# Second layer of a two-layer encoder: one 48-row product for the meta tokens' values of both halves, and two steps of the second half's norm issued one step later

## The chip, the cores and the metric

The kernel runs on one core of a Trainium2 chip. The metric is the device time of one execution in microseconds (us); the median of several runs is given.

## The reference

An encoder of two layers is applied to two requests (256 and 512 tokens of width 1024), each with the same 16 meta tokens put in front. Layer 0 mixes tokens by latent attention, layer 1 by windowed attention with 16 query heads in 4 groups; each is followed by a squared-ReLU MLP. Cut to what the change touches, the mixer of layer 1:

```python
qkv = x @ w_qkv                                   # x: 16 meta tokens + S tokens, width 1024
q = partial_rope(qkv[..., :1024]); k = partial_rope(qkv[..., 1024:1280]); v = qkv[..., 1280:]
km, vm = k[:, :16], v[:, :16]                     # meta keys and values: every query sees them
for each block of 128 queries:                    # own keys: 128 before to 128 after
    s = q_b @ [km, k_b].T / 8 + mask
    p = exp(s - m) / (sum(exp(s - m)) + exp(sink - m))
    out_b = p @ [vm, v_b]
```

Ahead of it stands the layer norm that ends layer 0: `y = (h - mean) * rsqrt(mean((h - mean)**2) + eps) * g + b`.

## The kernel before

All 800 columns (tokens of both requests, and the 16 meta tokens twice) are kept transposed, features on partitions, in two halves `hf` of 400 columns. Half 0 has its meta tokens in columns 0 to 15, half 1 in columns 128 to 143. Products are made in three matmuls each (`mm3`, lines 445 to 448): an operand is split into a high and a low part, and high x high, high x low and low x high are added in PSUM. The high part is a cast on ACT (L749, weights L761), the low part a subtraction on DVE (L751, weights L763).

The function `attention1` writes down the work from the last down-projection of layer 0's MLP to the output projection of layer 1 as tasks with a rough cost each; a list scheduler (`Plan`) puts them into an order for each engine by these costs, and each engine runs its list strictly in that order. So taking out or moving one task can shift others on any engine. In order:

- `down`: the down-projection's last part; PE, then DVE adds it to `acc` (L2094), and the sum over the eight feature chunks of a half, `ssb`, is gathered on POOL (L2098, L2101) and for the last two chunks on DVE (L2101).
- `layer_norm` gives three steps for each half. The mean step takes `ssb` through a product with a constant (PE L777), subtracts it (DVE L780), squares (ACT L782) and adds the squares up (POOL and DVE L786, DVE L788). The sums step brings the sums of squares onto rows (PE L795), ACT and DVE make 1/std of them (L799, L800). The scale step spreads that (PE L805), scales (DVE L810, ACT L813) and writes the halves' input `H[hf]` (`hb`) as high (ACT L749) and low part (DVE L751).
- `rope("q", c, hf, w)` projects a chunk `c` of queries in four steps of two feature chunks and turns it (DVE L2138, L2141, POOL L2143, DVE L2146, then the split L749 and L751) into `Q` (`q`); `rope("k", ...)` likewise for keys.
- `values(hf, wv)`: values of blocks of 128 tokens ("b", into `V`) and of the 16 meta tokens ("m", into `Vm`), 24 matmuls of 256 columns each. Here the activations are the stationary operand, so a product has as many rows as tokens. `Vm` gets its rows by four small copies on ACT (L2175) for each half.
- Attention in 24 items (head chunk `cp`, block `b`): `scores` (PE L2213, DVE L2222 adds the mask and takes maxima, L2230 and L2233, ACT L2237 exponentials with sums, L2240, DVE L2241, L2242, L2254, L2266 and POOL L2264 for two of four rows of heads each), `transposes` (PE L2283, L2291, ACT L2284, L2295), `outputs` (PE L2309, L2316). Names carry the item: `sma01` are the probabilities of `cp` 0, block 1; `es01` and `rs01` its sink exponentials and sums, `pk01` its meta columns. Beside the first items run the second half's values and the query chunks that are left.

PSUM has eight banks `wb_0` to `wb_7` in this stretch, taken in turn. The planned order of the norm steps is set in the loop that calls them:

Of the kernel before, what the change touches and what calls it, by code (L numbers as in the profile page):

```python
# [19 lines left out]
P = 128  # L20
D = 1024
NT = 800
META = 16
HALF = 400
# [349 lines left out]
def tile_encoder(ctx: ExitStack, tc: tile.TileContext, ins: dict, y):  # L374
    nc = tc.nc
    V, S, G = nc.vector, nc.scalar, nc.gpsimd
# [26 lines left out]
    def ps_w(name):  # L403
        return bank("w", name)
# [40 lines left out]
    def mm3(out, lh, ll, rh, rl, start, stop, **kw):  # L445
        nc.tensor.matmul(out, lh, rh, start=start, stop=False, **kw)  # L446
        nc.tensor.matmul(out, lh, rl, start=False, stop=False, **kw)  # L447
        nc.tensor.matmul(out, ll, rh, start=False, stop=stop, **kw)  # L448
# [57 lines left out]
    with ExitStack() as st:  # L506
        xp = pool("xp", side="right", stack=st)
        x = [xp.tile([P, 8, NT], F32R, tag=f"x{i}", name=f"x{i}") for i in range(2)]
# [187 lines left out]
        for o in IN_ORDER:  # L696
# [3 lines left out]
            for h in range(2):  # L700
                ps = ps_w(f"in{o}{h}")
# [11 lines left out]
                if o in (0, 1):  # L713
                    k = 2 * o + h
# [1296 lines left out]
    H = [[xs[hf].tile([P, 8, HALF], F32R, tag=f"hb{hf}{i}", name=f"hb{hf}{i}") for i in range(2)] for hf in range(2)]  # L2011
# [6 lines left out]
    at = {}  # L2018
# [41 lines left out]
    def attention1():  # L2060
        plan = Plan(
            {"wsp": NWSP, "wraw": WRAW, "wh": 1, "w": 8, "sqb": 6, "ssb": 1, "ssc": 1, "sqc": 6, "rt": 2, "sh": 1, "sma": 4, "smb": 3, "pta": 2, "ptb": 2,
             "rm": 4, "nm": 4, "rs": 4, "es": 4, "pk": 4, "ptm": 2, "mask": 1},
            {
                "wsp": spare([x for _, x in W.ready.values()]),
                "w": lambda k: ps_w(f"wb_{k}"),
                "sqb": lambda k: lnb.tile([P, HALF], F32, tag="sqb", name=f"sqb{k}", bufs=6),
                "sqc": lambda k: at["lnc"].tile([P, HALF], F32, tag="sqc", name=f"sqc{k}", bufs=6),
            },
# [42 lines left out]
        def rope(kind, c, hf, w):  # L2112
# [36 lines left out]

            return [lambda ks=ks: step(ks) for ks in (range(k, k + 2) for k in range(0, 8, 2))]  # L2150

        def values(hf, wv):

            steps = []
            for kind, i, a in [(("m", 0, 0), ("b", 0, 16), ("b", 1, 144), ("b", 2, 272)), (("b", 3, 0), ("m", 1, 128), ("b", 4, 144), ("b", 5, 272))][hf]:
                ps = new("w")
                m = META if kind == "m" else P

                def run(ps=ps, a=a, m=m):
                    for k in range(8):  # L2160
                        r = [wv[k // 4].t[:, x, (k % 4) * 256 : (k % 4 + 1) * 256] for x in range(2)]
                        mm3(ps.t[:m, :256], H[hf][0][:, k, a : a + m], H[hf][1][:, k, a : a + m], r[0], r[1], k == 0, k == 7)

                def step(kind=kind, i=i, ps=ps, run=run):
                    reads = [*wv, *both(*wv), *both(*[("H", hf, k) for k in range(8)])]
                    plan.task("PE", 24 * MM[256], run, reads=reads, writes=[ps], new=[ps], ends=[st2, st3] if hf == 0 else [st3])
                    if kind == "b":
                        plan.task("ACT", ACT(256), lambda: S.copy(at["V"][:, i], ps.t[:, :256]), reads=[ps, st1], writes=[("v", i)])
                        return
                    for ci, gi in ((0, 0), (0, 1), (1, 0), (1, 1)):  # L2170
                        x = 2 * ci + gi
                        rows = slice(32 * x, 32 * x + META)
                        src = lambda: ps.t[:META, :256].rearrange("p (a b c) -> p a b c", a=2, b=2)
                        plan.task(
                            "ACT", 290, lambda ci=ci, gi=gi, rows=rows: S.copy(at["Vm"][rows, i, :, ci, gi], src()[:, :, gi]),  # L2175
                            reads=[ps, st1], writes=[("vm", i, x)],
                        )

                steps.append(step)
            return steps  # L2180
# [245 lines left out]
        for n in range(len(ITEMS) + behind):  # L2426
            if n < len(ITEMS):
                cp, b = ITEMS[n]
# [29 lines left out]

    psum_phase(w=8)
    attention1()  # L2460
    sub.close()
    l1.close()
# [12 lines left out]
    ends = ExitStack()  # L2475
# [125 lines left out]
```

## Time and profile before

| | |
|---|---|
| median of 3 runs | 1750.49 us (1750.35 to 1751.98) |
| profiled execution | its own time is its span, 1750.7 us |
| granted PE clock, mean | 0.999 |
| busy: PE / DVE / ACT / POOL | 99% / 83% / 59% / 18% of the span |
| chain that ended last | PE 93%, DVE 4%, ACT 2% |

Rows of the profile in order of time give the start (us from the span's start), the duration, engine, line, operation, output<-inputs, shapes and, in brackets, how long the engine was idle ahead of it and whom it waited for. A PE row writes rows x columns: `128*16 128x256` has a stationary operand of 128 by 16 and a moving one of 128 by 256. Matmuls are pipelined, so a matmul's row is longer than its distance to the next one's start.

### The profile page before, as it was taken

How to read it: one execution, taken by the hardware profiler on the slowest of the kernel's cores; microseconds unless marked ns; L12 is line 12 of the kernel's file. 1: busy time of each engine (PE TensorE's matmuls, PEld its weight loads, DVE VectorE, ACT ScalarE, POOL GpSimd, SP SyncE). 2: the span in 40 equal slices, each digit the busy share in tenths (PEclk: the TensorE clock that was granted, in tenths of full speed). 3: DMA queues.
4: the chain of work that ended last, by engine and by line, in shares of the span. 5: the costliest groups of instructions: out<-in, count | busy, mean ns of one | idle time of the engine just before them, and what ended most of it. 6: DMA issues, size and time to landing. Idle time of an engine off the chain costs nothing.

```text
span 1750.7 us, 28797 instructions
## 1 busy us (share of the span) xinstructions
PE 1732.5 (99%) x10806; PEld 1628.4 (93%) x10806; DVE 1448.0 (83%) x2937; ACT 1026.2 (59%) x2172; POOL 309.2 (18%) x290
## 2 busy tenths in 40 slices
PE   9999999999999999999999999999999999999998
PEld 9999999989999999999999998788989889988996
DVE  6998889886977898889876877876877888888877
ACT  5577777774655446545643627775665456545652
POOL 0011111112220111111103232332211111211110
PEclk9999999999999999999999999999999999999999
DMA  7211001114311221222122231021311222222222
GB/s 243 77 41 32 22 20 42 35 42 140 121 61 49 73 72 62 73 72 73 61 89 83 81 104 38 21 66 61 121 49 49 80 65 73 73 72 73 73 68 89
DMA packets 39453, 124.16 MB, mean 71 GB/s; under 512 B 4752, under 2 KB 9744, under 8 KB 39184
## 3 DMA queue, kind: packets, MB, share of 16 engines
q1 hardware_dynamic: 39312, 122.31, 21.3%
q8 instruction: 85, 1.39, 0.3%
q14 instruction: 56, 0.46, 0.1%
HBM read 119.15 MB, written 3.15 MB: 70 GB/s over the span
## 4 chain that ended last, share of the span: by engine, by line
PE 93%; DVE 4%; ACT 2%; issue 0%; DMA 0%; POOL 0%; SPq 0%; DVEq 0%; ACTq 0%
PE w L447 18%; PE w L448 18%; PE w L446 18%; PE wb L446 4%; PE wb L447 4%; PE wb L448 4%; PE wa L446 3%; PE wa L448 3%; PE wa L447 3%; PE wa L1155 2%; PE sa L446 2%; PE wa L1122 2%; PE wb L2309 2%; PE sa L448 2%; PE sa L447 2%; PE wb L2291 1%
## 5 line engine op out<-in xcount | busy, mean ns | idle before, releaser
L1734 DVE TENSOR_TENSOR acc<-acc,w 128x400 f32<-128x400 f32 (+1 forms) x306 | 184.3, 618 | 35.3 <-PE w L448 33.3
L1466 DVE TENSOR_TENSOR h<-sq,h 128x384 fp32r<-128x384 f32 (+1 forms) x164 | 94.6, 589 | 19.4 <-ACT h L1464 18.9
L446 PE MATMUL w<-h,wsp 128*128 128x400 f32 x316 | 108.9, 345 | 0.0
L447 PE MATMUL w<-h,wsp 128*128 128x400 f32 x316 | 108.9, 345 | 0.0
L447 PE MATMUL w<-h,wspi 128*128 128x400 f32 x316 | 108.9, 345 | 0.0
L446 PE MATMUL w<-h,wspi 128*128 128x400 f32 x316 | 108.7, 344 | 0.0
L448 PE MATMUL w<-h,wspi 128*128 128x400 f32 x316 | 108.7, 344 | 0.0
L448 PE MATMUL w<-h,wsp 128*128 128x400 f32 x316 | 108.6, 344 | 0.0
L1464 ACT CAST h<-sq 128x384 fp32r<-128x384 f32 (+1 forms) x164 | 82.5, 515 | 20.5 <-POOL sq L1472 19.3
L1091 POOL TENSOR_TENSOR p<-p,rs 106x512 f32<-106x512 f32 (+1 forms) x40 | 44.7, 1117 | 253.5 <-DVE pk L1082 162.2
L448 PE MATMUL w<-wspi,h 128*128 128x512 f32 (+1 forms) x182 | 71.6, 393 | 0.0
L446 PE MATMUL w<-wspi,h 128*128 128x512 f32 (+1 forms) x182 | 71.5, 393 | 0.0
L447 PE MATMUL w<-wspi,h 128*128 128x512 f32 (+1 forms) x182 | 71.5, 393 | 0.0
L1645 ACT COPY sq<-w 128x400 f32<-128x400 f32 (+1 forms) x72 | 35.0, 486 | 61.0 <-PE w L448 61.0
L1064 ACT ACTIVATE p<-sa,nm,rq 106x528 f32<-106x528 f32 (+1 forms) x80 | 63.4, 792 | 10.5 <-DVE nm L1061 4.5
L1060 DVE TENSOR_REDUCE nm<-sa 106x1 f32<-106x528 f32 (+1 forms) x80 | 56.3, 704 | 13.8 <-PE sa L448 12.4
L446 PE MATMUL w<-wsp,h 128*128 128x512 f32 (+1 forms) x170 | 67.1, 395 | 0.0
L448 PE MATMUL w<-wsp,h 128*128 128x512 f32 (+1 forms) x170 | 66.8, 393 | 0.0
L447 PE MATMUL w<-wsp,h 128*128 128x512 f32 (+1 forms) x170 | 66.7, 393 | 0.0
L446 PE MATMUL sa<-k,q 128*106 128x264 f32 (+5 forms) x208 | 63.8, 307 | 2.8 <-issue 0.9
L446 PE MATMUL w<-t,wsp 128*128 128x384 f32 (+1 forms) x176 | 60.0, 341 | 0.0
L448 PE MATMUL w<-t,wsp 128*128 128x384 f32 (+1 forms) x176 | 59.9, 341 | 0.0
(823 smaller groups left out, 6173.7 us busy)
## 6 DMA issues: line engine op xcount, KB each, us to landing
wrawo<-in_w_o_dram SPq DMA_DIRECT2D x32, 512.0 KB, 3.3
wraw0d<-in_w2b_dram SPq DMA_DIRECT2D x24, 512.0 KB, 3.3
wraw1d<-in_w2b_dram SPq DMA_DIRECT2D x18, 512.0 KB, 3.4
wrawq<-in_w_q_dram SPq DMA_DIRECT2D x8, 512.0 KB, 3.3
xr<-in_xT_dram SPq DMA_DIRECT2D x16, 200.0 KB, 3.4
wraw<-in_w_qn_dram SPq DMA_DIRECT2D x8, 384.0 KB, 3.1
wx1d<-in_w2b_dram SPq DMA_DIRECT2D x6, 512.0 KB, 3.2
out_dram<-fo SPq DMA_DIRECT2D x11, 256.0 KB, 2.0
```

The source lines that it names most:

```text
L446: nc.tensor.matmul(out, lh, rh, start=start, stop=False, **kw)
L447: nc.tensor.matmul(out, lh, rl, start=False, stop=False, **kw)
L448: nc.tensor.matmul(out, ll, rh, start=False, stop=stop, **kw)
L1060: plan.task("DVE", DVE(528), lambda: V.tensor_reduce(nm.t[:qm, 0:1], v(), axis=AX.XY, op=ALU.max, negate=True), reads=[ps], writes=[nm], n ...
L1064: lambda: S.activation(P_().rearrange("p (a b) -> p a b", b=264), v(), AF.Exp, bias=nm.t[:qm, 0:1], scale=sc, accum_out=rs.t[:qm, 0:1]),
L1091: f = lambda row=row, r=r, w=w: G.tensor_tensor(row()[:, META:T], row()[:, META:T], r().to_broadcast([qm, w]), ALU.mult)
L1122: nc.tensor.transpose(ps.t[:, k * qm : (k + 1) * qm], src[k], ident[:qm, :qm])
L1155: nc.tensor.matmul(av[64 * e : 64 * e + 64, :n], vt.t[:, k, h0 + 64 * e : h0 + 64 * e + 64], PT.t[:, e, k, :n], start=k == 0, stop=False, ...
L1464: plan.task("ACT", 530, lambda: S.copy(d.t[:, 0], c.t[:, :n]), reads=[c], writes=[(d, "hi")], new=[d])
L1466: "DVE", 570, lambda: V.tensor_tensor(d.t[:, 1], c.t[:, :n], d.t.bitcast(F32)[:, 0], ALU.subtract),
L1734: f = lambda: V.tensor_tensor(z, z, ps.t[:, : z.shape[-1]], ALU.add)
L2309: nc.tensor.matmul(av[64 * gi : 64 * gi + 64, :256], at["V"][:, kbs[k][0], gc : gc + 64], PT.t[:, a : a + 256], start=k == 0, stop=False, ...
```

## The change

Before, half 0's `values` had products for its 16 meta tokens and three blocks, and half 1's for block 3, its 16 meta tokens and two blocks. Now half 0 has only its three blocks. A new helper `meta_along` copies, on POOL, the meta columns of `H[0]` and `H[1]`, high and low part, side by side into a stretch of the query tile `Q[1]` that is not yet in use (`along`): 16 columns of half 0 and, with the 16 in between that nobody reads, 32 of half 1, 48 columns for each of eight feature chunks. One product of 48 rows makes both halves' meta values, first of half 1's list, and its eight copies on ACT fill both parts of `Vm`. The mean step of the second half's norm is issued after the first product of `values(0)` rather than the second, its sums step after the second step of query chunk 2 rather than the first, and its scale step after the fourth rather than the third; `meta_along(1)` follows it.

```diff
+        def along(x):
+            return at["Q"][1][:, x, 1, HALF : HALF + 24 * META].rearrange("p (k m) -> p k m", m=3 * META)
+
+        def meta_along(hf):
+            a, b, d = ((0, META, 0), (128 - META, 128 + META, META))[hf]
+            for x, nm in enumerate(("hi", "lo")):
+                plan.task(
+                    "POOL", POOL(8 * (b - a)), lambda x=x: G.tensor_copy(along(x)[:, :, d : d + b - a], H[hf][x][:, :, a:b]),
+                    reads=[st1, *[(("H", hf, k), nm) for k in range(8)]], writes=[("Hm", nm)], ends=[st2, st3] if hf == 0 else [st3],
+                )
...
-            for kind, i, a in [(("m", 0, 0), ("b", 0, 16), ("b", 1, 144), ("b", 2, 272)), (("b", 3, 0), ("m", 1, 128), ("b", 4, 144), ("b", 5, 272))][hf]:
+            for kind, i, a in [(("b", 0, 16), ("b", 1, 144), ("b", 2, 272)), (("m", 0, HALF), ("b", 3, 0), ("b", 4, 144), ("b", 5, 272))][hf]:
                 ps = new("w")
-                m = META if kind == "m" else P
+                m = 3 * META if kind == "m" else P
...
-                        mm3(ps.t[:m, :256], H[hf][0][:, k, a : a + m], H[hf][1][:, k, a : a + m], r[0], r[1], k == 0, k == 7)
+                        l = [along(x)[:, k] if kind == "m" else H[hf][x][:, k, a : a + m] for x in range(2)]
+                        mm3(ps.t[:m, :256], l[0], l[1], r[0], r[1], k == 0, k == 7)
...
-                    for ci, gi in ((0, 0), (0, 1), (1, 0), (1, 1)):
+                    for i, ci, gi in [(i, ci, gi) for i in range(2) for ci in range(2) for gi in range(2)]:
                         x = 2 * ci + gi
                         rows = slice(32 * x, 32 * x + META)
-                        src = lambda: ps.t[:META, :256].rearrange("p (a b c) -> p a b c", a=2, b=2)
+                        r0 = 32 * i
+                        src = lambda r0=r0: ps.t[r0 : r0 + META, :256].rearrange("p (a b c) -> p a b c", a=2, b=2)
...
         for i, f in enumerate(values(0, wv)):
             f()
-            if i == 1:
+            if i == 0:
                 mean1()
+        meta_along(0)
         for c in range(2, 8):
             w = wq(c)
             for i, f in enumerate(rope("q", c, 0, w)):
                 f()
-                if (c, i) == (2, 0):
+                if (c, i) == (2, 1):
                     sums1()
-                if (c, i) == (2, 2):
+                if (c, i) == (2, 3):
                     scale1()
+                    meta_along(1)
```

From `values` on the line numbers of the new kernel are 12 or 13 higher (L2222 becomes L2235). PE's list loses 24 matmuls. Ahead of L777 it has one product of `values(0)` instead of two; between L795 and L805 it has two steps of query chunk 2, as before, but ahead of L795 two as well instead of one. In attention the 48-row product takes the place that block 3's product had, and block 3's the place of the 16-row one; PE's list is the same from there on. The other engines' lists at the two places:

**The norm, on POOL**, around the second half's sums `ssb1`; `shq` are turned queries, `vm1` is cleared, `sqb` are squares, `q1_1` takes the meta columns. Before:

```order
L2098 TENSOR_TENSOR ssb1_9939<-acc_845 128x400
L2101 TENSOR_TENSOR ssb1_9939<-ssb1_9939,acc_845 128x400 x2
L2143 TENSOR_TENSOR shq00_9951<-shq00_9951,sin10_9551 128x384
L2101 TENSOR_TENSOR ssb1_9939<-ssb1_9939,acc_845 128x400 x2
L2029 MEMSET vm1_10023 128x1024
L786 TENSOR_TENSOR sqb4_9764<-sqb4_9764,sqb3_9761 128x400
L786 TENSOR_TENSOR sqb5_9779<-sqb5_9779,sqb1_9740 128x400
L2143 TENSOR_TENSOR shq10_10127<-shq10_10127,sin10_9551 128x384
L2143 TENSOR_TENSOR shq20_10252<-shq20_10252,sin10_9551 128x384
```

and now:

```order
L2098 TENSOR_TENSOR ssb1_9933<-acc_845 128x400
L2101 TENSOR_TENSOR ssb1_9933<-ssb1_9933,acc_845 128x400 x4
L2029 MEMSET vm1_9999 128x1024
L2143 TENSOR_TENSOR shq00_9949<-shq00_9949,sin10_9551 128x384
L2159 COPY q1_1_9993<-hb00_9545 128x8x16
L2159 COPY q1_1_9993<-hb01_9546 128x8x16
L786 TENSOR_TENSOR sqb4_9764<-sqb4_9764,sqb3_9761 128x400
L786 TENSOR_TENSOR sqb5_9779<-sqb5_9779,sqb1_9740 128x400
L2143 TENSOR_TENSOR shq10_10126<-shq10_10126,sin10_9551 128x384
L2159 COPY q1_1_9993<-hb10_9547 128x8x32
L2159 COPY q1_1_9993<-hb11_9548 128x8x32
L2143 TENSOR_TENSOR shq20_10254<-shq20_10254,sin10_9551 128x384
```

All five sums stand ahead of the first rope product now; the copies of half 0 follow it and those of half 1 stand ahead of the third.

**The norm, on DVE**, from the first rope products to the subtraction of the mean (`wsp`, `wspi` are split weights). Before:

```order
L2138 TENSOR_TENSOR rtq10_9979<-wb_6_9677,cos10_9549 128x384
L2035 TENSOR_SCALAR nsink_10028<-sink_10027 128x16
L2101 TENSOR_TENSOR ssb1_9939<-ssb1_9939,acc_845 128x400 x2
L763 TENSOR_TENSOR wsp7_792<-wrawq2_9655,wsp7_792 128x1024
L2146 TENSOR_TENSOR rtq00_9949<-rtq00_9949,shq00_9951 128x384
L763 TENSOR_TENSOR wspi41_709<-wrawq3_9823,wspi41_709 128x1024
L780 TENSOR_TENSOR acc_845<-acc_845,wb_7_9692 128x400 x6
```

and now:

```order
L2138 TENSOR_TENSOR rtq10_9979<-wb_6_9677,cos10_9549 128x384
L2101 TENSOR_TENSOR ssb1_9933<-ssb1_9933,acc_845 128x400
L2035 TENSOR_SCALAR nsink_10004<-sink_10003 128x16
L2101 TENSOR_TENSOR ssb1_9933<-ssb1_9933,acc_845 128x400
L763 TENSOR_TENSOR wsp7_792<-wrawq2_9655,wsp7_792 128x1024
L780 TENSOR_TENSOR acc_845<-acc_845,wb_5_9658 128x400 x6
```

The rope sum and the second weight split have gone behind the sums of squares (L788).

**The start of attention, on ACT**: `v1` are values, `pta` and `ptm` transposed probabilities of blocks and of meta columns. Before:

```order
L2168 COPY v1_10022<-wb_0_9568 128x256
L2237 ACT_TABLE_LOAD
L2237 ACTIVATE sma00_10695,rs00_10749<-sma00_10695,nm00_10746 128x272 x4
L2240 ACTIVATE es00_10751<-es00_10751 128x4
L2175 COPY vm1_10023<-wb_4_9641 16x2x64 x4
L2237 ACTIVATE sma01_10716,rs01_10809<-sma01_10716,nm01_10775 128x272 x4
L2168 COPY v1_10022<-wb_6_9677 128x256
L2240 ACTIVATE es01_10827<-es01_10827 128x4
L2295 COPY pta00_10837<-wb_3_9623 128x512
L2284 COPY ptm00_10848<-wb_1_9585 128x128
L2295 COPY pta00_10837<-wb_2_9603 128x512
L2237 ACTIVATE sma02_10719,rs02_10887<-sma02_10719,nm02_10829 128x272 x4
```

and now:

```order
L2188 COPY vm1_9999<-wb_7_9692 16x2x64 x8
L2250 ACT_TABLE_LOAD
L2250 ACTIVATE sma00_10668,rs00_10731<-sma00_10668,nm00_10721 128x272 x4
L2253 ACTIVATE es00_10733<-es00_10733 128x4
L2180 COPY v1_9998<-wb_3_9623 128x256
L2180 COPY v1_9998<-wb_0_9568 128x256
L2297 COPY ptm00_10798<-wb_6_9677 128x128
L2308 COPY pta00_10801<-wb_2_9603 128x512
L2308 COPY pta00_10801<-wb_3_9623 128x512
L2250 ACTIVATE sma01_10725,rs01_10830<-sma01_10725,nm01_10808 128x272 x4
L2253 ACTIVATE es01_10819<-es01_10819 128x4
L2250 ACTIVATE sma02_10723,rs02_10866<-sma02_10723,nm02_10816 128x272 x4
```

The second item's exponentials have gone behind block 4's value copy and the copies of the first item's transposes. On DVE, the first of the two scalings of the second item's rows is followed by `L2243` and `L2246` of the fourth item and by `L2254` of the third, which reads `es02`, and only then by the second scaling; before, the two scalings stood together ahead of that.

More of the change, by code (lines that the diff above doesn't have):

```diff
@@ L2150, in rope, with run @@
             return [lambda ks=ks: step(ks) for ks in (range(k, k + 2) for k in range(0, 8, 2))]
+        def along(x):
[7 more added lines that the diff above has]
+                )
         def values(hf, wv):
             steps = []
-            for kind, i, a in [(("m", 0, 0), ("b", 0, 16), ("b", 1, 144), ("b", 2, 272)), (("b", 3, 0), ("m", 1, 128), ("b", 4, 144), ("b", 5, 272))][hf]:
+            for kind, i, a in [(("b", 0, 16), ("b", 1, 144), ("b", 2, 272)), (("m", 0, HALF), ("b", 3, 0), ("b", 4, 144), ("b", 5, 272))][hf]:
                 ps = new("w")
-                m = META if kind == "m" else P
-                def run(ps=ps, a=a, m=m):
+                m = 3 * META if kind == "m" else P
+                def run(ps=ps, a=a, m=m, kind=kind):
                     for k in range(8):
                         r = [wv[k // 4].t[:, x, (k % 4) * 256 : (k % 4 + 1) * 256] for x in range(2)]
-                        mm3(ps.t[:m, :256], H[hf][0][:, k, a : a + m], H[hf][1][:, k, a : a + m], r[0], r[1], k == 0, k == 7)
+                        l = [along(x)[:, k] if kind == "m" else H[hf][x][:, k, a : a + m] for x in range(2)]
+                        mm3(ps.t[:m, :256], l[0], l[1], r[0], r[1], k == 0, k == 7)
                 def step(kind=kind, i=i, ps=ps, run=run):
-                    reads = [*wv, *both(*wv), *both(*[("H", hf, k) for k in range(8)])]
+                    reads = [*wv, *both(*wv), *both(*[("H", hf, k) for k in range(8)]), *(both("Hm", ("q", 3, 1)) if kind == "m" else [])]
                     plan.task("PE", 24 * MM[256], run, reads=reads, writes=[ps], new=[ps], ends=[st2, st3] if hf == 0 else [st3])
@@ L2169, in step @@
                         return
-                    for ci, gi in ((0, 0), (0, 1), (1, 0), (1, 1)):
+                    for i, ci, gi in [(i, ci, gi) for i in range(2) for ci in range(2) for gi in range(2)]:
                         x = 2 * ci + gi
                         rows = slice(32 * x, 32 * x + META)
-                        src = lambda: ps.t[:META, :256].rearrange("p (a b c) -> p a b c", a=2, b=2)
+                        r0 = 32 * i
+                        src = lambda r0=r0: ps.t[r0 : r0 + META, :256].rearrange("p (a b c) -> p a b c", a=2, b=2)
                         plan.task(
-                            "ACT", 290, lambda ci=ci, gi=gi, rows=rows: S.copy(at["Vm"][rows, i, :, ci, gi], src()[:, :, gi]),
+                            "ACT", 290, lambda i=i, ci=ci, gi=gi, rows=rows, src=src: S.copy(at["Vm"][rows, i, :, ci, gi], src()[:, :, gi]),
                             reads=[ps, st1], writes=[("vm", i, x)],
```

## The prediction

> **What bounds the kernel.** I read the page's first and fourth part, then PE's instructions in order of time at the two places where the change moves work, then the other engines there.
>
> The page: span, PE's row, and the shares by engine of the chain that ended last.
>
> ```profile
> span 1750.7 us, 28797 instructions
> ...
> PE 1732.5 (99%) x10806; PEld 1628.4 (93%) x10806; DVE 1448.0 (83%) x2937; ACT 1026.2 (59%) x2172; POOL 309.2 (18%) x290
> ...
> PE 93%; DVE 4%; ACT 2%; issue 0%; DMA 0%; POOL 0%; SPq 0%; DVEq 0%; ACTq 0%
> ```
>
> PE is the bound, so a product taken out is worth its spacing on PE and nothing hides it. A busy PE is modelled; the spacing of starts tells its time. What is left is small waits, and the next rows (PE in order of time, second norm of the first layer) hold one.
>
> ```profile
> 976.15 0.28 PE L446 MATMUL wb<-wspi,hb 128*16 128x256 f32 x1
> 976.27 0.28 PE L447 MATMUL wb<-wspi,hb 128*16 128x256 f32 x1
> ...
> 981.79 0.83 PE L777 MATMUL wb<-ssb,part 128*128 128x400 f32 x2
> ...
> 989.00 0.34 PE L448 MATMUL wb<-hb,wsp 128*128 128x384 f32 x1
> 990.59 0.87 PE L795 MATMUL wb<-ones,sqb 128*100 128x1 f32 x8 [1.25 <-DVE sqb L788]
> ```
>
> From 976.15 to 981.79 stand 48 matmuls, 24 with 16 rows and 24 with 128: 5.64/48 = 0.1175 us each, and 0.12 between the first two. The rows of the product do not change the spacing. L448 at 989.00 would let the next start after about 0.18; L795 (row sums of squares) starts 1.59 later, so PE waits 1.41 us for the last sum of squares (L788).
>
> **Part 1, the product that goes.** The program has 24 matmuls fewer: 24 x 0.1175 = **-2.82 us**. The 48-row product stands where a 128-row one stood; both bounds (16 and 128 rows) give 0.1175, so it costs what its neighbours do.
>
> **Part 2, the norm.** DVE and POOL in order of time, with the 16-row product still in place:
>
> ```profile
> 976.44 1.02 POOL L2143 TENSOR_TENSOR shq<-shq,sin 128x384 f32<-128x384 f32 x1 [12.77 <-DVE shq L2141]
> 977.42 2.17 POOL L2101 TENSOR_TENSOR ssb<-ssb,acc 128x400 f32<-128x400 f32 x2
> ...
> 975.29 0.56 DVE L2138 TENSOR_TENSOR rtq<-wb,cos 128x384 f32<-128x384 f32 x1 [1.59 <-PE wb L448]
> 976.82 0.67 DVE L2035 TENSOR_SCALAR nsink<-sink 128x16 f32<-128x16 f32 x1
> 979.62 1.19 DVE L2101 TENSOR_TENSOR ssb<-ssb,acc 128x400 f32<-128x400 f32 x2 [2.13 <-POOL ssb L2101]
> ...
> 982.33 1.22 DVE L763 TENSOR_TENSOR wspi<-wrawq,wspi 128x1024 fp32r<-128x1024 f32 x1
> 983.46 2.96 DVE L780 TENSOR_TENSOR acc<-acc,wb 128x400 f32<-128x400 f32 x6
> ...
> 989.96 0.57 DVE L788 TENSOR_TENSOR sqb<-sqb,sqb 128x400 f32<-128x400 f32 x1
> ```
>
> PE reaches L777 one product earlier, at 976.15 + 2.82 = 978.97. Its input was ready only at 980.8 before, because POOL's last two sums stood behind a rope product that waited 12.77 us. Now POOL makes all its sums ahead of that product, and DVE's two sums follow its rope work of 975.3 to 976.8: two of 0.6, and the small L2035 of 0.67 between, end near 978.6. So L777 does not wait, with 0.4 us to spare. DVE then has one weight split (L763, 1.22; before it stood there too, with a second one and a rope sum behind it) and starts L780 when L777 is done, near 979.9. L780's start to L788's end took 990.53 - 983.46 = 7.07, so the squares are summed at 987.0. PE has between L777 and L795 what it had, 7.39 (981.79 to 989.18), and 6 matmuls of 384 columns more, 1.05: it comes at 978.97 + 8.44 = 987.4. The wait is gone, -1.41; the margin of 0.4 is thin, and I leave 0.1 of it: **-1.3 us**. Ends: all 1.41 goes, or all of it stays.
>
> The added copies on POOL: bounds are its small MEMSET and its 384-column product of 1.02 above; I take 0.5 each, as 128 and 256 columns lie between.
>
> ```profile
> 942.32 1.05 POOL L2101 TENSOR_TENSOR ssb<-ssb,acc 128x400 f32<-128x400 f32 x1 [1.13 <-DVE acc L2094]
> 959.79 3.88 POOL L2101 TENSOR_TENSOR ssb<-ssb,acc 128x400 f32<-128x400 f32 x2 [2.16 <-DVE acc L2094]
> 1053.98 0.11 POOL L2246 MEMSET sma<- 128x16 f32 x1
> ```
>
> The same addition takes 1.05 us alone and 1.94 beside a busy DVE, so the two engines get in each other's way. The copies of the first half come just where DVE makes the last two sums; if each held DVE up by its 0.5, L777 would wait 0.6 and PE would lose that. The Trainium skill, "SBUF — State Buffer", section "Who interferes with whom", says that a VectorE instruction with two SBUF inputs and a GpSimd one that reads SBUF exclude each other for the whole instruction. By that rule, with copies as long as the 1.02 row, L777 would wait some 1.7 and the sum would lose all of the gain of this part; the trace agrees with it on POOL's side (1.94), and shows nothing of a DVE held twice in a row.
>
> The copies of the second half stand on POOL ahead of a rope product and wait for the second half's H. PE needs that half first at the 400-column matmuls, and its last pair of chunks 18 matmuls on:
>
> ```profile
> 1003.40 1.86 DVE L751 TENSOR_TENSOR hb<-acc,hb 128x400 fp32r<-128x400 f32 x2
> 1003.87 0.34 PE L446 MATMUL wb<-hb,wspi 128*128 128x400 f32 x1
> ...
> 1007.17 0.34 PE L446 MATMUL wb<-hb,wspi 128*128 128x400 f32 x1
> ```
>
> Ready at 1005.26, read at 1007.17: 1.9 to spare. PE comes 4.2 earlier. DVE comes some 2.5 to 3 earlier, since it now has three weight splits of 1.2 between L788 and the first scaling. 0.2 to 0.7 is left: 0 lost, 0.6 at worst. The rope product behind the copies is delayed by about 1 us, and the bank that it empties is wanted again eight ropes later, of some 4.2 us each: 0. On SP's queue no DMA is added; the loads of the two rope tables and some weights change places by one, and nothing in these rows waits for a landing: 0.
>
> **Part 3, the start of attention.** PE's own order there is the old one, with the 48-row product where block 3's stood and block 3's where the 16-row one stood, so its arrival times stay. ACT's and DVE's order is new. First the busy time of each engine from 1051 to 1075, then rows of ACT, DVE, POOL and PE:
>
> ```profile
> 1051.00:1075.00 24.00, 24.00 (x219) 20.77 (x219) 17.01 (x77) 18.57 (x58) 6.19 (x11) 1.00 0.07 24
> ...
> 1055.71 0.37 ACT L2168 COPY v<-wb 128x256 f32<-128x256 f32 x1 [2.65 <-PE wb L448]
> 1057.24 1.28 ACT L2237 ACT_TABLE_LOAD   x1 [1.16 <-DVE nm L2230]
> ...
> 1060.58 0.19 ACT L2240 ACTIVATE es<-es 128x4 f32<-128x4 f32 x1
> 1060.67 1.03 ACT L2175 COPY vm<-wb 16x128 f32<-16x128 f32 x4
> ...
> 1064.13 0.58 ACT L2295 COPY pta<-wb 128x512 f32<-128x512 f32 x1
> 1064.60 0.27 ACT L2284 COPY ptm<-wb 128x128 f32<-128x128 f32 x1
> 1064.76 0.61 ACT L2295 COPY pta<-wb 128x512 f32<-128x512 f32 x1
> 1065.24 0.54 ACT L2237 ACTIVATE sma<-sma,nm 128x272 f32<-128x272 f32 x1
> ...
> 1067.27 0.20 ACT L2240 ACTIVATE es<-es 128x4 f32<-128x4 f32 x1
> ```
>
> ```profile
> 1060.80 0.16 DVE L2241 TENSOR_TENSOR rs<-rs,es 128x4 f32<-128x4 f32 x1 [1.70 <-ACT es L2240]
> 1066.78 0.81 DVE L2266 TENSOR_SCALAR sma<-sma,rs 128x272 f32<-128x272 f32 x2
> 1065.93 1.24 POOL L2264 TENSOR_TENSOR sma<-sma,rs 128x272 f32<-128x272 f32 x2 [2.83 <-DVE pk L2254]
> 1063.48 1.03 PE L2291 MATMUL wb<-ident,sma 128*128 128x128 f32 x8
> 1068.46 1.04 PE L2291 MATMUL wb<-ident,sma 128*128 128x128 f32 x8
> ```
>
> PE (the first 24.00) has no gap there. *First item.* Eight copies of meta rows (8 x 0.257 = 2.06) now stand ahead of the table load, from 1055.7 to 1057.8. The load waited for DVE's maxima until 1057.2; these now come early. So the load starts at 1057.8, 0.5 later than before, and so do the exponentials and DVE's rs: 1061.3. DVE scales the rows between masks and ends near 1063.5 to 1064.0; PE's second four transposes want them at 1063.48 + 0.44 = 1063.9. I take +0.1, from 0 to 0.5.
>
> *Second item.* Its exponentials ran from 1061.7 before. Now ACT has ahead of them block 4's value copy, which waits for PE until 1063.5, and the three copies of the first item's transposes. Those take 0.47, 0.16 and 0.48 and ended at 1065.24; without the queue ahead of them at 1065.1. Four exponentials take 1067.27 - 1065.24 = 2.03, so es of item 2 is done at 1067.2 and es of item 3, straight after, at 1069.3. DVE scales one of its two rows of item 2, then has rs of item 3 in its queue, which waits for that es, and only then the other row: es to rs 0.22, scaling 0.36, near 1069.95. PE wants that row at 1068.46 + 0.44 = 1068.9. **+1.1 us** of wait where there was 0.9 to spare. Ends: 0, if PE were late anyway, and 1.7, if POOL's scaling (1.24 for two) collides too. In PE's time the third item gets the same 1.1 of respite, so I charge nothing after it; from the second item of heads on, the order is nearly as before.
>
> **The sum.** -2.82 - 1.3 + 0.1 + 1.1 = -2.9 us. The profiled span is 1750.7, so 1747.8 there; the median of the runs stands 0.2 under it (1750.49), which gives **1747.6 us**, 0.17% faster. I call 0.2% (3.5 us) what a measurement of this kernel can tell from no change.
>
> **Rivals.**
> - *Attention does not wait.* If ACT's queue is slack enough, part 3 is 0 and the time is 1750.5 - 4.1 = 1746.4. For it: PE had no gap there before, and ACT was idle for 5.4 of the 24 us. Against it: the exponentials of item 2 are bound by PE's own transposes of item 1, which no engine can hasten. 0.27.
> - *The norm's wait stays*, by copies that block DVE or a late sum: 1747.6 + 1.3 = 1748.9. The rule on the shared port gives this result. For it the margin of 0.4, against it POOL's earlier sums. 0.15.
> - *Slower.* Lateness of ACT does not heal: each item's exponentials stand behind the transposes of the one before, and each costs 1.1 again. Four items eat the 4.1 of parts 1 and 2; from the seventh on the kernel is slower by over 0.2%, and twelve give 1750.5 - 4.1 + 13.2 = 1759.6. Against it: an item is 5 us of PE and ACT's row of the span is 59%. 0.04.
>
> **How the numbers follow.** My forecast has 0.50, with 1747.0 to 1748.5 for its own range; 0.04 is for what I do not see. Low end: no wait in attention and all of 1.41, less a little, 1746.0. High end: the norm's wait stays and attention takes its upper price, 1747.6 + 1.3 + 0.5 = 1749.4. Faster by over 0.2% (under 1747.0): nearly all of 0.27 and a sixth of the forecast, 0.35. Slower 0.04. The same 0.61.
>
> **What would show it.** In the profile after: 24 matmuls fewer and the 48-row ones 0.12 apart; no idle time ahead of L795; ACT idle for some 1.8 us ahead of block 4's value copy; a PE wait of about 1.1 us for DVE's scaling in the transposes of the second item, and none at the third. I am wrong if ACT gets its exponentials out earlier, if L777 becomes a waiter, or if the first 400-column rope waits for H.

## The result

The changed kernel has a median of 1747.52 us (16 runs, 1747.20 to 1749.43); the kernel before, run beside it, 1751.96 us (16 runs, 1750.35 to 1753.78). The ratio is 0.9977, 95% interval 0.9971 to 0.9984: 0.23% faster, with the time 0.1 us from the forecast. One run of a kernel further down, at a granted clock of 0.556, took 2828.26 us and is left out there.

The medians differ by 4.4 us, where the forecast had 2.9, and the median of before is not the 1750.49 of its first three runs. Both kernels' times stand in groups:

| | lowest group | second | third |
|---|---|---|---|
| before | 1750.35 to 1750.56 (6 runs) | 1751.85 to 1752.24 (8) | 1753.73 to 1753.78 (2) |
| changed | 1747.20 to 1747.88 (13) | 1749.23 to 1749.43 (3) | none |

Group against group the change is worth about 3.0 us (medians of the lowest ones 1750.47 and 1747.46); the rest is how many runs fell into which group. Whether the change has a part in that is not shown: over all rounds the kernel before was in its lowest group in 54 of 102 runs and the changed one in 20 of 27, but two of the kernels below that are edits of the kernel before (`norm only` and `norm only, clean`) were there in 17 of 22. The two profiles shown are from different groups as well, so they have to be compared with the start of the program taken out. The table below does that: the start of the same PE instruction in two profiles, second minus first, as a median over a stretch (us of the first profile's axis).

| profiles | 600 to 900 | 1003 to 1040 | 1070 to 1090 | 1600 to 1745 | change without the start |
|---|---|---|---|---|---|
| before, changed | -1.98 | -6.28 | -5.05 | -5.11 | **-3.13** |

-1.98 is there from 20 us on, far ahead of anything that the change touches. Product and norm then give 4.30, attention takes 1.23 back, and the rest of the program moves by 0.06.

### The profile after

The page's span, PE's row and the chain by engine:

```profile
span 1745.6 us, 28754 instructions
...
PE 1728.5 (99%) x10782; PEld 1625.0 (93%) x10782; DVE 1449.6 (83%) x2937; ACT 1027.3 (59%) x2172; POOL 311.7 (18%) x294
...
PE 93%; DVE 3%; ACT 2%; issue 0%; DMA 0%; SPq 0%; DVEq 0%; ACTq 0%
```

PE has 24 matmuls fewer and is still the bound. The norm, PE, then DVE, then POOL in order of time:

```profile
974.17 0.28 PE L446 MATMUL wb<-wspi,hb 128*128 128x256 f32 x1
...
977.00 0.83 PE L777 MATMUL wb<-ssb,part 128*128 128x400 f32 x2
...
985.47 0.78 PE L795 MATMUL wb<-ones,sqb 128*100 128x1 f32 x8
```
```profile
974.84 0.60 DVE L2101 TENSOR_TENSOR ssb<-ssb,acc 128x400 f32<-128x400 f32 x1
...
975.54 0.56 DVE L2101 TENSOR_TENSOR ssb<-ssb,acc 128x400 f32<-128x400 f32 x1
...
977.87 2.98 DVE L780 TENSOR_TENSOR acc<-acc,wb 128x400 f32<-128x400 f32 x6 [0.53 <-PE wb L777]
...
984.38 0.57 DVE L788 TENSOR_TENSOR sqb<-sqb,sqb 128x400 f32<-128x400 f32 x1
```
```profile
974.96 1.29 POOL L2159 CAST q<-hb 128x128 fp32r<-128x128 f32 x2
...
999.33 0.40 POOL L2159 CAST q<-hb 128x256 fp32r<-128x256 f32 x1 [10.09 <-ACT hb L749]
1000.22 0.67 POOL L2159 CAST q<-hb 128x256 fp32r<-128x256 f32 x1 [0.49 <-DVE hb L751]
```

One product of 24 matmuls (974.17 to 977.00) stands ahead of L777 instead of two. DVE's last sum ends at 976.10, 0.9 before L777 needs it. L795 has no bracket: the squares are summed at 984.95, PE comes at 985.47.

The start of attention, ACT, then PE, then DVE and POOL at the second item:

```profile
1049.29 2.12 ACT L2188 COPY vm<-wb 16x128 f32<-16x128 f32 x8 [2.23 <-PE wb L448]
1051.43 1.28 ACT L2250 ACT_TABLE_LOAD   x1
...
1057.25 0.37 ACT L2180 COPY v<-wb 128x256 f32<-128x256 f32 x1 [1.90 <-PE wb L448]
1057.52 0.27 ACT L2297 COPY ptm<-wb 128x128 f32<-128x128 f32 x1
1057.80 1.15 ACT L2308 COPY pta<-wb 128x512 f32<-128x512 f32 x2
1058.84 0.52 ACT L2250 ACTIVATE sma<-sma,nm 128x272 f32<-128x272 f32 x1
...
1062.99 0.20 ACT L2253 ACTIVATE es<-es 128x4 f32<-128x4 f32 x1
```
```profile
1046.28 0.32 PE L446 MATMUL wb<-wsp,q 128*48 128x256 f32 x1
...
1048.98 0.28 PE L448 MATMUL wb<-wspi,q 128*48 128x256 f32 x1
...
1057.16 1.16 PE L2304 MATMUL wb<-ident,sma 128*128 128x128 f32 x8
...
1062.27 0.32 PE L2304 MATMUL wb<-ident,sma 128*128 128x128 f32 x1
1062.76 0.55 PE L2304 MATMUL wb<-ident,sma 128*128 128x128 f32 x3 [0.17 <-POOL sma L2277]
1063.81 0.63 PE L2304 MATMUL wb<-ident,sma 128*128 128x128 f32 x4 [0.51 <-DVE rs L2255]
...
1066.94 1.04 PE L2304 MATMUL wb<-ident,sma 128*128 128x128 f32 x8
```
```profile
1062.12 0.60 DVE L2243 SCALAR_TENSOR_TENSOR nm<-rm,nsink 128x4 f32<-128x4 f32 x1
...
1062.75 0.56 DVE L2246 TENSOR_TENSOR es<-sink,nm 128x4 f32<-128x4 f32 x1
1063.24 0.15 DVE L2254 TENSOR_TENSOR rs<-rs,es 128x4 f32<-128x4 f32 x1
1063.31 0.35 DVE L2279 TENSOR_SCALAR sma<-sma,rs 128x272 f32<-128x272 f32 x1
...
1061.95 1.35 POOL L2277 TENSOR_TENSOR sma<-sma,rs 128x272 f32<-128x272 f32 x2 [4.56 <-DVE pk L2267]
```

The 48-row matmuls stand (1048.98 - 1046.28)/23 = 0.117 us apart. The first item's eight transposes take 1.16 instead of 1.04. The second item's eight, 0.109 apart without a wait, lose 0.38 after the first and 0.67 after the fourth; the third item's run through.

The first of the two waits is for POOL's scaling (1061.95), which stands behind the second item's row sums `rs01` and so behind exponentials that ACT starts at 1058.84, after block 4's value copy (idle 1.90 for PE) and the three copies of the first item's transposes. The second wait is for DVE's second scaling of this item (1063.31 to 1063.66). The bracket names L2255, which only ended last; no transpose of this item reads it. Ahead of that scaling in DVE's list stands L2254 of the third item, which reads `es02`, done on ACT at 1062.99 + 0.20 = 1063.19. L2243 and L2246 of the fourth item stand there too, and they took 0.60 and 0.56 while POOL scaled, against 0.14 to 0.17 wherever POOL was idle. They came to an end with `es02`, so each of the two reasons alone would have held the scaling to about 1063.3. That scaling sets the whole delay: without a wait the fifth transpose would have started at 1062.27 + 4 x 0.109 = 1062.71, and it started at 1063.81.

### The profile page after: what moved, and what is told of

The parts are those of the page before. It is cut to its first block, busy times and chain, and to the rows that moved or that the text cites. A ratio compares the mean times of both kernels' runs of the same rounds, so it can differ in the third digit from the quotient of the medians.

```text
span 1745.6 us, 28754 instructions
## 1 busy us (share of the span) xinstructions
PE 1728.5 (99%) x10782; PEld 1625.0 (93%) x10782; DVE 1449.6 (83%) x2937; ACT 1027.3 (59%) x2172; POOL 311.7 (18%) x294
## 3 DMA queue, kind: packets, MB, share of 16 engines
q8 instruction: 84, 1.38, 0.3%
## 4 chain that ended last, share of the span: by engine, by line
PE 93%; DVE 3%; ACT 2%; issue 0%; DMA 0%; SPq 0%; DVEq 0%; ACTq 0%
PE w L447 18%; PE w L448 18%; PE w L446 18%; PE wb L446 4%; PE wb L447 4%; PE wb L448 4%; PE wa L446 3%; PE wa L448 3%; PE wa L447 3%; PE wa L1155 2%; PE sa L446 2%; PE wa L1122 2%; PE wb L2322 2%; PE sa L448 2%; PE sa L447 2%; PE wb L2304 1%
```

## Experiments

The "change" of each is the table's last column: the column ahead of it minus the first, against the kernel named. It ends with PE's last matmuls.

| kernel | against | 600 to 900 | 1003 to 1040 | 1070 to 1090 | 1600 to 1745 | change |
|---|---|---|---|---|---|---|
| changed, again | changed | +1.85 | +1.85 | +1.84 | +1.84 | 0.0 |
| before, 10 warm-ups | before | -2.16 | -2.16 | -2.16 | -2.12 | 0.0 |
| before, 3 warm-ups | before | -0.41 | -0.42 | -0.42 | -0.38 | 0.0 |
| product twice | changed | -0.06 | -0.06 | +2.61 | +2.58 | +2.64 |
| norm only | before | -0.28 | -0.61 | -0.61 | -0.62 | -0.34 |
| norm only, clean | before | -2.18 | -3.23 | -3.23 | -3.30 | -1.12 |
| early norm | changed | +0.35 | +1.05 | +0.29 | +0.71 | +0.36 |
| exponentials first | changed | -0.19 | -0.19 | -1.11 | -1.09 | -0.90 |
| product second | changed | +0.06 | +0.06 | -0.95 | +0.15 | +0.09 |
| exponentials first, 10 warm-ups | changed | +0.34 | +0.34 | -0.59 | -0.48 | -0.82 |

### The groups: the program's start

The changed kernel itself, without an edit.

> The changed kernel itself, as the measure for the other runs on the same chip. Theory: its times fall into groups, most at 1747.2 to 1747.9 and some 1.7 to 2.0 above, as the kernel before has at 1750.2 to 1750.8 and 1752.0 to 1752.8; group against group the change is worth 2.9 to 3.1 us. Rival: the change is worth 4 us or more, and the groups of the two kernels do not correspond.

Seven runs at 1747.45 to 1747.89, four at 1749.23 to 1749.71; beside it the kernel before had 15 of 33 at 1750.26 to 1750.80, 12 at 1751.96 to 1752.64 and 6 at 1753.66 to 1753.99. Lowest against lowest: 1747.70 against 1750.47, 2.8 us; second against second (1749.35, 1752.16) 2.8, just under what was expected. The ratio was 0.9980 (0.9972 to 0.9989). The profiled run (1749.39) is of the upper group, and the same kernel's two profiles differ by 1.85 at 600 us already and by no more at the end. PE's first rows, of this run and then of the profile above:

```profile
4.56 1.35 PE L446 MATMUL in<-x,wsp 128*128 128x400 f32 x2
5.71 0.54 PE L447 MATMUL in<-x,wsp 128*128 128x400 f32 x1
6.04 0.54 PE L448 MATMUL in<-x,wsp 128*128 128x400 f32 x1
...
8.78 0.54 PE L448 MATMUL in<-x,wsp 128*128 128x400 f32 x1
9.12 0.87 PE L447 MATMUL in<-x,wsp 128*128 128x400 f32 x2
```
```profile
4.33 1.31 PE L446 MATMUL in<-x,wsp 128*128 128x400 f32 x2
5.44 0.48 PE L447 MATMUL in<-x,wsp 128*128 128x400 f32 x1
5.75 0.34 PE L448 MATMUL in<-x,wsp 128*128 128x400 f32 x1
5.93 0.35 PE L446 MATMUL in<-x,wsp 128*128 128x400 f32 x1
```

And the busy times from 6 to 9 us, again of this run and then of the profile above (first the length of the stretch, then PE with its matmuls; PEclk is the third number from the right):

```profile
6.00:9.00 3.00, 3.00 (x10) 2.73 (x10) 0.96 (x3) 1.29 (x4) 0.00 (x0) 1.00 0.98 315
```
```profile
6.00:9.00 3.00, 2.89 (x16) 2.55 (x15) 1.55 (x4) 1.77 (x4) 0.00 (x0) 1.00 0.96 324
```

The same matmul of 400 columns takes 0.333 us in one execution until about 10 us, and 0.18 from 5.75 in the other: 10 against 16 of them in 3 us. The column of the granted clock reads 1.00 in both, but the clock record in the trace, from which it is made, begins only at 10.21 us in this run and at 5.71 in the profile above, both times with full clock; the column counts the time ahead of the record as full. The next two vary the warm-up products that fill PE ahead of these rows.

```diff
-    for _ in range(7):
+    for _ in range(10):    # and range(3)
         nc.tensor.matmul(warm[:, :P], part, part, start=True, stop=True)
```

> The kernel before with ten instead of seven warm-up products of 128 columns at the program's start. In the profile of before the projection's first matmuls of 400 columns stood 0.333 us apart from 5.57 to 10, in the profile of the changed kernel 0.18 apart from 5.75; the times of both kernels fall into groups 1.65 to 1.9 us apart. Theory: the groups are that pace, which follows a gap of PE ahead of 5.57; with PE busy until about 5.4 the pace is 0.18 to 0.19 from the first matmul on, and all runs fall within 0.6 us, near the fastest group of before (1750.0 to 1750.9). Rival: the groups come from elsewhere (transfers, the end of the program); the times still spread over 1.6 us or more.

> The kernel before with three warm-up products instead of seven: PE is then idle from about 2.5 until the first projection matmul near 4.3. Theory: the groups are the pace of the first projection matmuls, and PE's work ahead of them decides it; so no run falls into the lowest group (1750.2 to 1750.8), nearly all stand at 1752.0 or above, and the profile shows matmuls 0.333 apart until 10 or later. Rival: the groups have nothing to do with the warm-up; then a third or more of the runs are at 1750.2 to 1750.8.

With ten, 10 of 11 runs were at 1750.24 to 1750.88 and one at 1752.77; the profile had 0.18 from 5.74 on. With three, none of 11 was in the lowest group (1751.77 to 1753.44), and the profile showed the row below. All twelve kept traces fit. In the four that are of an upper group (before, changed again, norm only, before with 3 warm-ups) the clock record begins at 9.95 to 10.21 us and 0.333 lasts to 9.8 to 10.1; in the eight others the record begins at 4.54 to 7.24 and 0.333 is over by 7.3. So the two lower groups are the pace of the first matmuls, and PE's work ahead of them shifts how often the fast one comes. With seven warm-ups either comes, and what decides it in one execution is not shown; nor is the third group, of which there is no profile. That one run with ten warm-ups still came 2 us late stays open.

```profile
4.26 0.70 PE L446 MATMUL in<-x,wsp 128*128 128x400 f32 x1 [1.55 <-ACT x L463]
```

The Trainium skill, "TensorE: Matmul & The Clock Gate", Part 1, says that the array runs at half its clock until a window of about 3.4 us has been busy, and that the window runs freely. The traces agree in the paces (its 400 columns at 1.2 GHz are 0.333). An estimate from its window, half of 3.4, gives 1.7 us for one more window at half pace; the groups lie 1.6 to 2.2 apart by their medians. A step of this size shows in the clock records, where full clock lasts 1733.97 or 1737.38 us in all twelve traces, 3.41 apart.

### The product: made twice

```diff
-                    for k in range(8):
+                    for k in [*range(8)] * (2 if kind == "m" else 1):
```

> The changed kernel with the 48-row product made twice over the same accumulator (the second pass starts it afresh), which adds 24 matmuls of 48 rows and 256 columns and leaves every other engine's order as it is. Theory: nothing hides a product on PE, so it costs 24 x 0.1175 = 2.8 us against the changed kernel at the same start. Rival: attention's waits of 1.05 in the second item take part of it up, since ACT and DVE get that much respite, and it costs only 1.7 to 2.0.

Lowest group 1749.96 to 1750.61 (8 runs) against 1747.45 to 1747.89: 2.5 us between their medians (1750.22, 1747.70). In the profile everything is later by 2.67 from the product on, and by 2.64 at the end. Nothing hides it and the attention waits do not take it up; the expected 2.8 was 0.15 too high. Around attention the orders of ACT, DVE and POOL are those of the changed kernel here.

### The norm: alone, alone and clean, and undone

On the kernel before, the later steps without the new product:

```diff
-                if (c, i) == (2, 0):
+                if (c, i) == (2, 1):
                     sums1()
-                if (c, i) == (2, 2):
+                if (c, i) == (2, 3):
                     scale1()
```

> The kernel before with only the sums and scale steps of the second half's norm one step later; both products for the meta tokens stay. DVE's order up to the sum of squares is that of before (rope sum and second weight split ahead of L780), and PE has six matmuls of 384 columns (1.05 us) more ahead of L795. Theory: the wait ahead of L795 falls from 1.41 to 0.3 or 0.4 and the kernel gains 1.0 to 1.1, nothing else moves. Rival: the squares are late because the engine they run on follows PE, and the wait stays at 1.2 or more.

Nine of 11 runs at 1750.26 to 1750.77, the place of before's lowest group; by the profile 0.34 faster up to PE's last matmul. A miss. The idle time ahead of L795 fell only from 1.25 to 0.94 (PE's row, then ACT's in order of time):

```profile
991.05 0.87 PE L795 MATMUL wb<-ones,sqb 128*100 128x1 f32 x8 [0.94 <-DVE sqb L788]
```
```profile
983.77 1.02 ACT L782 ACTIVATE sqb<-acc 128x400 f32<-128x400 f32 x2 [1.10 <-DVE acc L780]
985.21 0.38 ACT L2168 COPY v<-wb 128x256 f32<-128x256 f32 x1 [0.42 <-PE wb L448]
985.48 1.82 ACT L782 ACTIVATE sqb<-acc 128x400 f32<-128x400 f32 x4
```

PE was given six more matmuls ahead of L795 (1.05 us), but the planner also moved block 1's value copy on ACT from behind the sixth square to behind the second, where it waits for PE, and the squares were summed 9.49 after L777's start (981.50 to 990.99) instead of 8.74 (981.79 to 990.53): 0.75 of the 1.05 was spent again. The next kernel moves that one copy behind all the squares, by its cost in the plan.

```diff
-                        plan.task("ACT", ACT(256), lambda: S.copy(at["V"][:, i], ...
+                        plan.task("ACT", 900 if hf == 0 else ACT(256), lambda: S.copy(at["V"][:, i], ...
```

> The norm alone once more: the kernel before with the sums and scale steps one step later, and the planner's cost of half 0's value copies raised to 900 ns. Against the norm-only kernel one instruction moves: ACT's copy of block 1's values, which waited for PE until 985.21 in the middle of the squares, now stands behind all of them. Theory: that copy made the squares 0.75 late and so ate 0.75 of the 1.05 that the later step gives; without it the wait ahead of L795 falls to 0.1 to 0.4 and the kernel is 0.9 to 1.1 faster than before at the same start of the program. Rival: the squares are late because DVE and ACT are fully booked there; then the wait stays at 0.8 or more and the gain at 0.3.

1749.51 to 1750.08 in the lowest group (8 of 11), 0.7 under that of before; by the profile -1.05 at the norm and -1.12 at PE's last matmul. The two measures differ since in both norm-only kernels 0.3 is lost again behind that: from the start of PE's last matmul to the end of the span 8.70 and 8.71 us pass, against 8.42 before and 8.43 in the changed kernel. The cause of that stays open. At the norm, ACT's order is the only one that differs between the two norm-only traces, so the copy's place was the cause there. The idle time is left at 0.20:

```profile
988.41 0.87 PE L795 MATMUL wb<-ones,sqb 128*100 128x1 f32 x8 [0.20 <-DVE sqb L788]
```

The opposite edit, in the changed kernel (steps back at `(2, 0)` and `(2, 2)`):

> The changed kernel with the sums and the scale step of the second half's norm back after the first and third step of query chunk 2. PE then reaches L795 six matmuls of 384 columns (1.05 us) earlier; DVE's order around the norm stays that of the changed kernel, where the squares were summed at 984.95 and L795 started at 985.47. Theory: the later step is needed for part of the wait only, so an idle time of 0.5 to 0.7 comes back ahead of L795 (not the 1.41 of before, since the rope sum and the second weight split have gone behind the squares). The planner also puts the second item's exponentials ahead of the first item's transposed copies here, so by the theory that their place makes PE's two waits of 0.38 and 0.67 in the second item's transposes, these shrink to under 0.3 together. Net against the changed kernel: 0.2 to 0.7 faster. Rival: the later step alone removed the wait; then 1.2 to 1.5 stands ahead of L795 and the kernel is slower than the changed one by 0.3 or more. Second rival: the waits in the transposes are collisions of POOL and DVE, and stay at 1.0.

```profile
985.36 0.87 PE L795 MATMUL wb<-ones,sqb 128*100 128x1 f32 x8 [0.45 <-DVE sqb L788]
```

The norm came out 0.70 slower and attention 0.76 faster, both as expected; the planner had put the second item's exponentials ahead of the first item's copies here too. But the whole was not faster, which is a miss: 1747.37 to 1748.13 in the lowest group, +0.36 by the profile, because 0.4 more was lost in the norm after attention (1245 to 1256). That loss was not followed up. For the change it follows that the later step is worth 0.7 next to the new product. The other half of the wait had gone with the order on DVE and POOL that the product alone leaves: here L780 starts 0.87 after L777 (978.22 and 977.35) instead of 1.67 before (983.46 and 981.79), and the squares are summed 7.96 after it instead of 8.74.

### Attention: the exponentials first

```diff
-                            "ACT", 290, lambda i=i, ci=ci, gi=gi, rows=rows, src=src: S.copy(at["Vm"] ...
+                            "ACT", 600, lambda i=i, ci=ci, gi=gi, rows=rows, src=src: S.copy(at["Vm"] ...
```

> The changed kernel with the planner's cost of each of the eight meta copies raised from 290 to 600 ns; the work is the same, PE's and POOL's orders are the same, ACT's and DVE's change at the start of attention: the second item's exponentials start ahead of block 4's value copy and of the first item's transposed copies, and DVE's two scalings of the second item's rows stand together again. Theory: PE's waits of 0.38 and 0.67 in the second item's transposes came from that place in ACT's queue; both go, 0.8 to 1.05 us faster than the changed kernel. Rival: PE is late there for POOL's scaling, which collides with DVE's; then 0.4 or more of wait stays and the gain is under 0.6.

```profile
1055.29 0.52 ACT L2250 ACTIVATE sma<-sma,nm 128x272 f32<-128x272 f32 x1
...
1057.07 0.37 ACT L2180 COPY v<-wb 128x256 f32<-128x256 f32 x1 [1.16 <-PE wb L448]
1057.34 0.52 ACT L2250 ACTIVATE sma<-sma,nm 128x272 f32<-128x272 f32 x1
...
1058.96 0.56 ACT L2308 COPY pta<-wb 128x512 f32<-128x512 f32 x1
```
```profile
1056.98 1.38 PE L2304 MATMUL wb<-ident,sma 128*128 128x128 f32 x8
...
1062.31 1.04 PE L2304 MATMUL wb<-ident,sma 128*128 128x128 f32 x8
```

With the higher cost the planner puts the second item's exponentials ahead on ACT, and on DVE the two scalings of that item ahead of what stood between them. Nine of 10 runs at 1746.69 to 1746.98, the fastest kernel here. The exponentials end ahead of the transposed copies, and the second item's eight transposes take 1.04, without a wait; the first item's take 1.38, 0.3 of wait. The same work in PE's same order is 0.90 faster by the profile, so the waits came from the order on ACT and DVE; the edit does not tell the two apart. The lowest groups differ by 0.6 to 0.8 only: a run's own time is 2.09 to 2.21 above its span here and 1.86 to 1.97 in the changed kernel. The next kernel goes after those 0.3 as well, with the product second in the list:

```diff
-(("m", 0, HALF), ("b", 3, 0), ("b", 4, 144), ("b", 5, 272))
+(("b", 3, 0), ("m", 0, HALF), ("b", 4, 144), ("b", 5, 272))
```

> The changed kernel with the cost of the meta copies at 600 ns as in the run that put the second item's exponentials first, and the 48-row product second in half 1's list instead of first. The eight copies then stand behind the first item's exponentials instead of ahead of their table load. Theory: the 2.06 us of copies made the first item's exponentials late and left a wait of 0.2 to 0.3 in the first item's transposes; it goes as well, and the kernel is 1.1 to 1.4 faster than the changed one. Rival: the copies now push the second item's exponentials back again, and 0.4 or more of wait shows in the second item's transposes; then it is no faster than the run with the cost alone, or slower by 0.2 to 0.5.

The first item's transposes took 1.04, without a wait. Yet at 1090 us it was only 0.95 + 0.06 = 1.0 ahead of the changed kernel, 0.1 more than the kernel above, where 1.1 to 1.4 was expected. Then it lost all of it between 1095 and 1122, in the transposes of later items, of which this is one:

```profile
1098.52 0.33 PE L2296 MATMUL wb<-ident,pk 128*128 128x128 f32 x1
1099.20 1.09 PE L2304 MATMUL wb<-ident,sma 128*128 128x128 f32 x8 [0.36 <-ACT ptm L2297]
```

1747.52 to 1748.12 in the lowest group: no gain. Neither theory had the place: the copies did not push the second item back, but the orders that the planner made up to seven items further on came out worse; which instruction's place it was is not shown. Last, the two edits that helped, together (cost 600, ten warm-ups):

> The changed kernel with the cost of the meta copies at 600 ns (second item's exponentials first) and ten warm-up products instead of seven: the two edits that gained, together. Theory: 0.7 to 1.0 under the lowest group of the changed kernel, 1746.5 to 1747.1, and nearly all runs in that group. Rival: the warm-up moves the order of the first stage and costs 0.3 or more, and the times still fall into two groups with a third or more in the upper one.

Ten runs at 1746.88 to 1747.61. No run of the upper group, but a start 0.5 later than with the exponentials first alone, so it beats the changed kernel by 0.5 to 0.7 in the lowest group (0.7 to 1.0 was expected) and is no better there than that edit by itself.

## Why the prediction was right

- *Product, -2.82.* Right. PE reaches L777 2.8 earlier (-1.98 becomes -4.79 there), 48 rows cost what 128 do, and making it twice cost 2.64.
- *Norm, -1.3.* Right in mechanism; it gave 4.30 - 2.82 = 1.48. All of the 1.41 went, where the forecast left 0.1 of it, and L795 without a wait keeps PE 0.64 instead of 0.73. PE came 0.5 after the last sum of squares, 0.4 was forecast. The margin at L777 was 0.9 and not 0.4: DVE's two sums ended at 976.10, where the same point of the prediction's axis was 978.6 (976.6 after the start's 1.98), mostly since the small L2035 took 0.26 and not 0.67.
- *The rule on the shared port.* The forecast gave "the norm's wait stays" 0.15. DVE's sums took 0.60 and 0.56 while POOL's two copies ran from 974.96 to 976.25. Each sum began ahead of its copy (974.84 and 974.96, 975.54 and 975.55), and the copy ended 0.15 after it. By the Trainium skill, "SBUF — State Buffer", "Who interferes with whom", the two exclude each other; the trace agrees, but it was POOL that was held, and L777 did not wait. Where POOL began first, DVE was held: L2243 and L2246 above, and the second L751 at 999.36 beside the copy of 999.33, which took 0.79 where the one ahead of it took 0.58.
- *The second half's H, 0.* Right. DVE's low part was ready at 998.87 + 1.28 = 1000.15 and PE read it at 1000.88, 0.7 later, where the forecast left 0.2 to 0.7.
- *Attention, +0.1 and +1.1.* Right. The net is 1.23 by the table; the first item's transposes lost 0.1, the second item's waits are 0.38 + 0.67 = 1.05. The cause was the forecast one, DVE's second scaling behind the third item's `es02` (forecast 1069.3 less the 6.28 of the table, 1063.0; measured 1063.19). POOL's scaling, which the forecast did not name, made the first of the two waits, inside the same delay. That L2243 and L2246 were held by POOL was not forecast either, and cost nothing more only because `es02` came at the same time. The forecast called PE the first 24.00 of its row of busy times; that is the length of the stretch, and PE the second, with the same value. It healed at the third item, and the rival of lateness that grows did not come.
- *ACT idle for some 1.8 ahead of block 4's value copy*: 1.90.
- *The sum, -2.9*: -3.13 by the profiles, 2.8 to 3.0 by groups.
- *The base.* This step was wrong without harm. The forecast took the profiled execution's time for its span (1750.7) and set the median 0.2 under it. A run's own time is 1.65 to 2.2 above its span in all but one of the runs (1747.53 and 1745.6, 1749.39 and 1747.5, 1752.18 and 1750.4), so that profile was of a run near 1752.5, in the second group, and the three runs' median of the lowest. The gain was then subtracted from a time of the lowest group, and most runs of the changed kernel fell there. So the difference was forecast, but that the time came out within 0.1 us is in part luck.
- *The range.* The medians' 4.4 us is more than any case of the forecast gave. It came from the groups, which were to be seen in the three runs (1750.35, 1750.49, 1751.98) and in PE's first rows; the prediction looked at neither. The groups also carried the ratio past the 0.2% that the forecast took for no change, to which it gave 0.61; group against group the change is 0.17%. By the medians alone the rival "attention does not wait" (4.1 faster) would look right; PE's waits of 1.05 rule it out.

## What to carry to other kernels

Where an engine is the bound, price a removed instruction by the spacing of starts, and then walk the other engines' new order: the planner gave back 0.9 of 4.3 here by the place of one item's exponentials and scalings, and in the norm-only kernel 0.75 of 1.05 by one copy. A cost in the plan that was no measured time (600 for a copy of 0.26) won it back, but the next such move lost 1.0 seven items later, so each order has to be measured to its end. Before two profiles are subtracted, compare them where nothing was changed: 2.0 of the 5.1 us here were the program's start.

## What had not been expected of the hardware

- The first matmuls of 400 columns run 0.333 or 0.18 us apart, by the execution, and the trace's record of full clock begins at 9.95 to 10.21 or at 4.54 to 7.24 us; this makes groups of times 1.6 to 2.2 us apart. The column of the granted clock shows 1.00 even ahead of that record. Ten warm-up products instead of seven kept 10 of 11 runs in the lowest, three kept none.
- DVE's and POOL's instructions held each other, and the one that began first was not held: DVE's L2243, of 4 elements, took 0.60 inside POOL's scaling and 0.15 to 0.17 without POOL, and POOL's copies took 0.64 and 0.71 behind DVE's sums, where a later one of twice the size that began first took 0.40.
- ACT's table load started 0.02 after the last copy (1049.29 + 2.12 and 1051.43), and cost 1.28.
